# First key columns, gate tiles, RWKV's first operands and the last attention units, in a two-layer hybrid backbone step

## The chip, the cores and the metric

The kernel runs on one core of one Trainium2 chip. The metric is the device time of one launch in microseconds, the median of several runs.

## The reference, cut to what matters

One inference step of a two-layer backbone (width 1024) over 256 context tokens and 1024 latent tokens, 1280 rows in all, in float32.

```python
for i in range(2):                      # layer 0 even, layer 1 odd
    m = silu(cond) @ mod_w[i] + mod_b[i]            # shift, scale, gate (3 x 1024)
    h = rms_norm(x, norm_g[i]) * (1 + scale) + shift
    x = x + gate * mixer_i(h)
# even mixer: z = h @ w_in, split into
#   A: attention, 8 query heads of 64, 2 key heads, softmax over 512 cached
#      + 1024 latent + 256 context keys (context rows see only context)
#   B: RWKV-7, 8 heads of 64, both directions, each branch times a SiLU gate
#   concat(A, B) @ w_out
# odd mixer: gated linear attention, both directions, gate, @ w_out
# finally rms_norm
```

The change lies in the even mixer: in the passage from its projections to attention and RWKV, and in the order of attention's last pieces.

## The kernel before

**Stages.** Layer 0 first projects the normalised rows (`project_on`, L667) into queries, keys, values, gates and RWKV inputs, and stores all of them in DRAM (`qh_d`, `kh_d`, `vo_d`, `ga_d`, `gb_d`, `ws_d`, `vt_d`). Each float32 product of the projections is three products of split halves. Then the mixers run side by side: RWKV in 40 segments (`rwkv_seg`, L1381: 4 head pairs, 5 stretches of 256 rows, 2 directions), attention in 12 units (4 query-head pairs p4, 3 row groups g) and the remaining modulation columns as filler. Output projection, layer 1 and its output projection follow.

**Who sets the order.** The kernel carries its own planner, `Sched` (from L100). Every operation is a call that the planner holds back. Tasks are generators, grouped in streams (`drive`, L411). The planner estimates for the first instructions of each task when they could start, and issues the earliest (L470). At equal times the lower rank goes first: a stream's place in the list of `drive`, or, for streams with a share, a rank that they have in common and that grows with the TensorE time they have used. A stream with a lead is treated as if its start were that much earlier, except on SyncE. The engines then run their instructions in the order so fixed, and SyncE issues every DMA in that order; a transfer that must wait holds up all behind it. In what follows SPq is SyncE's issue queue. `get` (L369) takes a tile from a tag's free tiles and blocks until there is one, `put` gives it back, `until` waits on a condition in the planner's order, `then` sets a flag in it.

**Rooms.** SBUF is reused by stage. `room_attn` (L1239) waits until the projections but for the gates are done, makes the tiles of attention (KA and KB for each of two key heads, 1792 columns; VO; QA and QB, 4 each; `mw` and `m4`, one each, for modulation), loads the first head's KA, fills KB's other half on POOL (row 64 of KB is ones, the row that carries minus the row maximum in QB), loads `sT` and sets `attn`. `room_rwkv` (L1310) waits for the last gate's products and for two PSUM banks of the projections, makes the tiles of RWKV and its masks and constants, fills them (POOL memsets, then identity blocks into LL and Z by whichever of ScalarE and VectorE the planner prefers), and sets `rwkv`, for which every `rwkv_seg` waits before it takes its tiles and loads its operands AR, BK and Vs (256, 256 and two times 64 KB).

**Gates.** `gated` (L785) evicts a projected gate through a tile `gt` (two of them, L726): tanh on ScalarE, a product on VectorE, a store. `mod_cols` (L551), in the mixer stage called by `mods` (L1300) with 256 columns at a time, loads 1 MB of `mod_w` into `mw` and, for gate columns, a row of `mod_b` into a tile `gt`; it multiplies by sT, and stores the gate row.

**Attention.** `maxima` (L1678) goes through the units in order. Each unit has two halves (one query head each). For every half it loads QA (two issues) and QB, multiplies blocks of 128 queries with KA in chunks of 512 keys (`cw`), reduces each product's row maximum on VectorE, transposes the maxima on TensorE, negates them on ScalarE and sends them into row 64 of QB. A unit's maxima may run at most some 13 key tiles ahead of attention (`SLACK`, L1665). `attend` (L1718) starts when both halves are ready: score products KA x QA + KB x QB, exp on ScalarE, product with VO, sums on VectorE or POOL. It has one PSUM bank `po`, so one unit accumulates at a time. Units 10 and 11 are head pair 3 with the two groups of 512 latent rows. `room_norm` (L2306) waits for all units.

The streams of the mixers, with (tasks at once, share, lead):

```python
mixers = (((rwkv_norm(p, sts[p]) for p in range(4)), 1),
          ((rwkv_seg(...) for p in range(4) for step in range(5) for d in range(2)), 4, 2000, 0.15),
          (attention(maxima), 1, 60),
          (attention(attend), 2, 150), ([keys()], 1), ([mods()], 1))
```

Of the kernel before, what the change touches and what calls it, by code (L numbers as in the profile page):

```python
# [486 lines left out]
def tile_hybrid_dit_step(ctx: ExitStack, tc: tile.TileContext, I, C, O):  # L487
# [63 lines left out]
    def mod_cols(i, c0, n, bank, row, ready=lambda: True):  # L551
# [4 lines left out]
        for a in range(NK // nk):  # L556
# [19 lines left out]
        m4 = yield from get("m4", False)  # L576
# [14 lines left out]
        else:  # L591
            PE.matmul(p[0:2, :], lhsT=msel, rhs=m, start=True, stop=True)
            V.tensor_tensor(b[0:2, 0:n], p[0:2, :], b[0:2, 0:n], ALU.add)
            V.tensor_scalar(m[0:2, :], b[0:2, 0:n], 0.5, 0.0, ALU.mult, ALU.add)
            put(row, b)
# [122 lines left out]
    flags = dict(left=0, gates=0, attn=False, keys=0, rwkv=False, mods=False, normed=False, gla=False, gl=False, units=0, weights=0, lr=0, begun=0, ra=False)  # L718
# [21 lines left out]
    def layer0():  # L740
# [153 lines left out]
        def mods(n):  # L894

            yield from sch.until(lambda: loads[0] >= (5 if n % 2 else 1))
            yield from mod_cols(0, n * 512, 512, "a", "xr", lambda: modded[0] and modded[1])
# [341 lines left out]
    def room_attn():  # L1239
# [37 lines left out]
    def load_keys(v, x):  # L1277

        src = kh_d[64 * v:64 * v + 64, 0, :]
        if x == 0:  # L1280
            for h in range(2):
                D.dma_start(out=KA[v][64 * h:64 * h + 64, :].bitcast(F32), in_=kh_d[64 * v:64 * v + 64, h, :])
        else:
            D.dma_start(out=KB[v][0:64, :].bitcast(F32), in_=src)

    def keys():

        yield from sch.until(lambda: flags["attn"])
        def done():
            flags["keys"] += 1  # L1290

        load_keys(0, 1)
        D.dma_start(out=VO.rearrange("p t v d -> p t (v d)"), in_=vo_d)
        sch.then(done)
        yield from sch.until(lambda: attended[1] >= 2)
        for x in range(2):
            load_keys(1, x)
        sch.then(done)

    def mods():  # L1300
        yield from sch.until(lambda: flags["attn"])
        for i, c0 in ((0, 2 * DM), (1, 0)):
            for c in range(c0, 3 * DM, 256):
                yield from mod_cols(i, c, 256, "b", "gt")
# [5 lines left out]
    def room_rwkv():  # L1310
# [15 lines left out]
        D.dma_start(out=m1f, in_=C["k_m1"].rearrange("p (d c) -> p d c", d=2))  # L1326
        id16 = rc.tile([P, P], F16, name="id16")
# [10 lines left out]
        slots("y", 2, [P, T], pool=rn)  # L1338
        slots("AR", 3, [P, 3, 4, 64])
        slots("BK", 3, [P, 2, 4, 64])  # L1340
        slots("Vs", 3, [P, 2, 2, 64])
# [1133 lines left out]
```

## Time and profile before

| | us |
|---|---|
| median of 3 runs | 2081.95 (2080.56 to 2083.43) |
| the profiled execution | 2079.51 |
| its span, first to last instruction | 2077.7 |
| mean granted clock of TensorE | 0.987 |
| TensorE busy | 1991.9 (96%) |
| VectorE, ScalarE, POOL busy | 1453.5, 1007.2, 296.1 |

The profile was taken on one execution. PE is TensorE's products, PEld its weight loads, DVE VectorE, ACT ScalarE, SP SyncE. In it the projections of layer 0 end at 509.9 us, RWKV and attention run from there to about 1300, the rest is the output projection and layer 1. All operations go through one helper, so every row has the line of that helper (L357), and rows are told apart by their tiles: hhi, hlo, whi, wlo are the projections, AR to Xr RWKV, QA, KA, QB, KB, VO, mx, mr, pt, acc attention, mw, m, gate modulation. `pj` and `a` are PSUM banks.

### The profile page before, as it was taken

Reading aid. Unit: us, or ns where it says so; the run is one execution under the profiler, and the core shown is the slowest. Engines: PE = TensorE matmul, PEld = TensorE weight load, DVE = VectorE, ACT = ScalarE, POOL = GpSimd, SP = SyncE. Lnnn points to the kernel's source line nnn. Section 1 sums busy time; section 2 is a strip of 40 time slices with the busy share of each in tenths; the row PEclk is TensorE's granted clock in tenths of the full one; section 3 lists DMA queues with packets and bytes.
Section 4 is the critical chain, followed back from the end, with each engine's and each line's share of the span. In section 5 each row is a group of like instructions: output and inputs, shape, how many; then the busy total and the mean of one; then the engine's idle time right before and its main releaser. Section 6 shows DMA issues by size and latency. Waiting matters only on the chain.

```text
span 2077.7 us, 38540 instructions
## 1 busy us (share of the span) xinstructions
PE 1991.9 (96%) x14876; PEld 1554.9 (75%) x14876; DVE 1453.5 (70%) x2877; ACT 1007.2 (48%) x2181; POOL 296.1 (14%) x388
## 2 busy tenths in 40 slices
PE   6999999998899999999999998999999999999998
PEld 3878687886577777777777774788788888888886
DVE  4677866777887888888988888464575656564455
ACT  4455653553556646665656654153445454542111
POOL 2010200004221112111110111010121111110011
PEclk9999999999999989999999999999999999999999
DMA  8224342436613242223223214353101011115653
GB/s 300 71 102 160 132 164 90 166 102 217 196 49 112 65 143 74 77 78 120 67 80 92 70 55 139 117 172 90 35 22 56 29 49 34 44 33 171 188 173 111
DMA packets 215431, 220.61 MB, mean 106 GB/s; under 512 B 16512, under 2 KB 161264, under 8 KB 215248
## 3 DMA queue, kind: packets, MB, share of 16 engines
q1 hardware_dynamic: 215248, 218.15, 33.2%
q8 instruction: 117, 1.92, 0.4%
q14 instruction: 66, 0.54, 0.1%
HBM read 150.68 MB, written 67.39 MB: 105 GB/s over the span
## 4 chain that ended last, share of the span: by engine, by line
PE 55%; DVE 11%; issue 2%; ACT 2%; DMA 1%; SPq 0%; POOL 0%; POOLq 0%; DVEq 0%; ACTq 0%
PE a L357 31%; PE pj L357 24%; DVE QQ L357 2%; DVE mx L357 1%; DVE LL L357 1%; ACT QQ L357 1%; DVE TT L357 1%; DVE Z L357 1%; DVE dec L357 1%; DVE gt L357 1%; DVE y L357 0%; DVE GR L357 0%; DVE KX L357 0%; DVE acc L357 0%; DVE TR L357 0%
## 5 line engine op out<-in xcount | busy, mean ns | idle before, releaser
L357 PE MATMUL pj<-hhi,whi 128*128 128x512 f32 (+1 forms) x672 | 241.0, 361 | 2.6 <-DVE whi L357 1.4
L357 PE MATMUL pj<-hlo,whi 128*128 128x512 f32 (+1 forms) x672 | 241.2, 361 | 0.6 <-DVE hlo L357 0.6
L357 PE MATMUL pj<-hhi,wlo 128*128 128x512 f32 (+1 forms) x672 | 240.2, 359 | 1.6 <-DVE wlo L357 1.6
L357 PE MATMUL a<-h1hi,whi 128*128 128x512 f32 (+3 forms) x448 | 162.2, 363 | 0.0
L357 PE MATMUL a<-h1lo,whi 128*128 128x512 f32 (+3 forms) x448 | 161.7, 362 | 0.4 <-DVE h1lo L357 0.4
L357 PE MATMUL a<-h1hi,wlo 128*128 128x512 f32 (+1 forms) x424 | 153.7, 362 | 0.0
L357 PEld LDWEIGHTS pj<-hhi,whi 128*128 128x128 f32 x672 | 128.7, 192 | 26.4 <-issue 3.7
L357 PEld LDWEIGHTS pj<-hlo,whi 128*128 128x128 f32 x672 | 129.0, 192 | 23.8 <-issue 5.8
L357 PEld LDWEIGHTS pj<-hhi,wlo 128*128 128x128 f32 x672 | 128.8, 192 | 24.0 <-issue 4.1
L357 POOL TENSOR_TENSOR acc<-acc,pt 128x512 f32<-128x512 f32 (+1 forms) x57 | 72.4, 1278 | 379.2 <-ACT pt L357 221.9
L357 DVE TENSOR_TENSOR acc<-acc,pt 128x512 f32<-128x512 f32 (+1 forms) x127 | 93.1, 757 | 13.9 <-ACT pt L357 10.2
L357 PE MATMUL a<-pt,VO 128*64 128x512 f32 (+1 forms) x368 | 95.6, 602 | 0.3 <-ACT pt L357 0.3
L357 PE MATMUL a<-woh,oh 128*128 128x512 f32 (+1 forms) x248 | 91.8, 370 | 2.8 <-DVE oh L357 2.8
L357 PEld LDWEIGHTS a<-h1hi,whi 128*128 128x128 f32 (+1 forms) x448 | 83.3, 186 | 13.3 <-issue 0.4
L357 PEld LDWEIGHTS a<-h1lo,whi 128*128 128x128 f32 (+1 forms) x448 | 83.3, 186 | 13.2 <-DVE h1lo L357 0.8
L357 PE MATMUL a<-woh,ol 128*128 128x512 f32 (+1 forms) x248 | 91.5, 370 | 1.7 <-DVE ol L357 1.7
L357 PE MATMUL a<-wol,oh 128*128 128x512 f32 (+1 forms) x248 | 91.5, 369 | 0.0
L357 PEld LDWEIGHTS a<-h1hi,wlo 128*128 128x128 f32 x424 | 80.1, 189 | 11.2 <-DVE wlo L357 0.4
L357 POOL TENSOR_SCALAR sq<-sq 128x1 f32<-128x1 f32 x70 | 19.6, 280 | 479.6 <-ACT gt L357 195.3
L357 ACT ACTIVATE pt<-pj 128x512 f32<-128x512 f32 (+1 forms) x123 | 68.7, 593 | 35.4 <-PE pj L357 31.8
L357 DVE TENSOR_REDUCE mx<-pj 128x1 f32<-128x512 f32 (+1 forms) x117 | 74.2, 651 | 2.1 <-PE pj L357 2.1
L357 DVE TENSOR_REDUCE mx<-a 128x1 f32<-128x512 f32 x91 | 59.9, 672 | 9.6 <-PE a L357 9.5
(505 smaller groups left out, 5285.3 us busy)
## 6 DMA issues: line engine op xcount, KB each, us to landing
mw<-in_mod_w SPq DMA_DIRECT2D x24, 1024.0 KB
ws<-wk SPq DMA_DIRECT2D x32, 512.0 KB
wst<-in_ev_w_in SPq DMA_DIRECT2D x26, 512.0 KB
wst<-in_od_w_in SPq DMA_DIRECT2D x24, 512.0 KB
AR<-ws SPq DMA_DIRECT2D x40, 256.0 KB
BK<-ws SPq DMA_DIRECT2D x40, 256.0 KB
wst<-o SPq DMA_DIRECT2D x14, 512.0 KB
Vs<-vt SPq DMA_DIRECT2D x80, 64.0 KB
```

What stands on the lines that cost most here:

```text
L357: r = f(*a, **k)
```

## The change

Five edits. The first key head's KA is loaded in two parts: columns 0 to 511 in `room_attn`, the rest in `keys` after the first unit's first queries have been issued (`asked`); the first score may go before the rest (`ka`). `sT` is loaded after that, and `mods` waits for it. KB of the second head is filled when it is loaded, not at the start. `mod_cols` no longer takes a tile for the `mod_b` row but uses the second half of its own `m4` tile, which for gate columns it takes before the products. In `room_rwkv` the tiles y, AR, BK and Vs are made right after the masks, and a flag `segs` lets the segments load their operands then; their work still waits for `rwkv`. The fills of LL and Z go to ScalarE. Attention's units 10 and 11 form a stream of their own with a lead of 0.15 and no share.

```diff
-    def mod_cols(i, c0, n, bank, row, ready=lambda: True):
+    def mod_cols(i, c0, n, bank, ready=lambda: True):
...
             if a == 0 and c0 >= 2 * DM:
-                b = yield from get(row, False)
-                D.dma_start(out=b[0:2, 0:n], in_=I["mod_b"][i:i + 1, c0:c0 + n].to_broadcast([2, n]))
+                m4 = yield from get("m4", False)
+                b = m4[0:2, n:2 * n]
+                D.dma_start(out=b, in_=I["mod_b"][i:i + 1, c0:c0 + n].to_broadcast([2, n]))
...
-        m4 = yield from get("m4", False)
+        if c0 < 2 * DM:
+            m4 = yield from get("m4", False)
...
-            put(row, b)
...
 (room_attn)
-        load_keys(0, 0)
-        for v in range(2):
-            G.memset(KB[v][64:128, :].bitcast(F32), 0.0)
-            G.memset(KB[v][64:65, :].bitcast(F32), 1.0)
-        D.dma_start(out=sT.rearrange("p k c -> p (k c)"), in_=sT_d)
+        load_keys(0, 0, slice(0, 512))
+        fill_keys(0)
...
 (keys)
-        yield from sch.until(lambda: flags["attn"])
...
+        yield from sch.until(lambda: flags["attn"] and asked[0] >= 1)
+        load_keys(0, 0, slice(512, PAST + T))
+        sch.then(first)                       # sets flags["ka"]
+        D.dma_start(out=sT.rearrange("p k c -> p (k c)"), in_=sT_d)
+        sch.then(lambda: flags.__setitem__("sT", True))
         load_keys(0, 1)
         D.dma_start(out=VO.rearrange("p t v d -> p t (v d)"), in_=vo_d)
         sch.then(done)
         yield from sch.until(lambda: attended[1] >= 2)
+        fill_keys(1)
         for x in range(2):
             load_keys(1, x)
...
     def mods():
-        yield from sch.until(lambda: flags["attn"])
+        yield from sch.until(lambda: flags["sT"])
...
 (room_rwkv, after gmask, zmask and m1f are loaded)
+        slots("y", 2, [P, T], pool=rn)
+        slots("AR", 3, [P, 3, 4, 64])
+        slots("BK", 3, [P, 2, 4, 64])
+        slots("Vs", 3, [P, 2, 2, 64])
+
+        def loads():
+            flags["segs"] = True
+        sch.then(loads)
         id16 = rc.tile([P, P], F16, name="id16")
...
-                linear(x[:, :, 0, :], ident.unsqueeze(1).to_broadcast([P, 4, P]), -1.0)
+                S.mul(x[:, :, 0, :], ident.unsqueeze(1).to_broadcast([P, 4, P]), -1.0)
...
-                    copy(fv(x[:, 0, d * h:d * h + 1], ...), fv(id16[:, d * h:d * h + 1], ...))
+                    S.copy(fv(x[:, 0, d * h:d * h + 1], ...), fv(id16[:, d * h:d * h + 1], ...))
...
 (rwkv_seg)
-        yield from sch.until(lambda: flags["rwkv"])
+        yield from sch.until(lambda: flags["segs"])
...
         for e in range(2):
             D.dma_start(out=Vs[64 * e:64 * e + 64].rearrange("p j h k -> p j (h k)"), ...)
+        yield from sch.until(lambda: flags["rwkv"])
...
 (maxima, after the two QA issues)
+            if i == hh == 0:
+                def issued():
+                    asked[0] += 1
+                sch.then(issued)
...
                 for c in range(nch):
+                    yield from sch.until(lambda: c == 0 and k0 == 0 or flags["ka"])
...
-              (attention(attend), 2, 150), ([keys()], 1), ([mods()], 1))
+              (attention(attend, 0, 10), 2, 150), (attention(attend, 10), 2, None, 0.15), ([keys()], 1), ([mods()], 1))
```

## Rows read from the trace of the kernel before

**Rows 1.** The page's part 1: busy time of each engine, its share of the span, and the number of instructions.

```profile
PE 1991.9 (96%) x14876; PEld 1554.9 (75%) x14876; DVE 1453.5 (70%) x2877; ACT 1007.2 (48%) x2181; POOL 296.1 (14%) x388
```

**Rows 2.** The view by stretches of 5 us around the passage from the projections to the mixers. Columns: stretch (us), its length, busy time and number of instructions of PE, PEld, DVE, ACT and POOL, mean granted clock of TensorE, mean busy share of the DMA engines, GB/s.

```profile
505.00:510.00 5.00, 4.90 (x22) 3.74 (x20) 0.66 (x2) 0.23 (x1) 3.72 (x3) 1.00 0.96 296
510.00:515.00 5.00, 0.04 (x1) 0.07 (x1) 0.00 (x0) 0.00 (x0) 4.98 (x8) 0.81 1.07 233
515.00:520.00 5.00, 5.00 (x12) 3.69 (x12) 4.24 (x8) 0.00 (x0) 5.00 (x10) 0.50 0.97 306
520.00:525.00 5.00, 1.99 (x18) 0.68 (x17) 4.84 (x17) 2.59 (x7) 0.50 (x2) 0.84 1.09 307
525.00:530.00 5.00, 4.59 (x21) 2.48 (x13) 4.97 (x16) 1.94 (x8) 2.69 (x10) 0.82 0.49 173
530.00:535.00 5.00, 2.72 (x21) 1.13 (x22) 5.00 (x12) 0.20 (x1) 0.00 (x0) 0.86 1.08 358
535.00:540.00 5.00, 4.62 (x42) 3.67 (x40) 3.59 (x10) 2.75 (x7) 2.27 (x3) 0.80 0.73 214
540.00:545.00 5.00, 3.24 (x32) 2.38 (x33) 4.18 (x11) 3.15 (x7) 0.59 (x1) 1.00 0.70 226
```

**Rows 3.** The timeline: start and length in us, engine, line, operation, output <- inputs, shapes, number; in brackets the engine's idle time just before and what ended it. The first keys and queries, the first score, the first row maximum.

```profile
506.25 1.11 SPq L357 DMA_DIRECT2D KA<-kh  x2
508.03 1.08 SPq L357 DMA_DIRECT2D QA<-qh  x2
...
514.96 0.77 PE L357 MATMUL a<-KA,QA 128*128 128x512 f32 x1 [5.06 <-DMA QA<-qh]
...
515.76 0.69 DVE L357 TENSOR_REDUCE mx<-a 128x1 f32<-128x512 f32 x1 [7.86 <-PE a L357]
```

**Rows 4.** The DMA view. The first line is what the engines moved in 40 equal slices (1.125 us each) of the stretch from 500 to 545 us; the others are issues by kind in it or in the stretch from 490 to 600: number, KB each.

```profile
GB/s 15 107 382 322 337 379 273 248 236 230 175 240 287 204 204 350 384 381 356 351 260 240 372 209 0 53 334 389 363 366 304 340 309 224 27 146 87 153 323 383
...
KA<-kh SPq DMA_DIRECT2D x2, 448.0 KB
...
sT<-sT_d SPq DMA_DIRECT2D x1, 128.0 KB
...
QA<-qh SPq DMA_DIRECT2D x8, 128.0 KB
...
AR<-ws SPq DMA_DIRECT2D x3, 256.0 KB
```

**Rows 5.** The timeline again: the key tiles' fills on POOL, the modulation's bias row into a gt tile, and the last gate's eviction on ScalarE.

```profile
502.35 6.43 POOL L357 MEMSET KB<- 64x1792 f32 x4
...
505.83 0.33 SPq L357 DMA_DIRECT2D gt<-in_mod_b  x1
...
520.41 0.60 ACT L357 ACTIVATE gt<-pj 128x512 f32<-128x512 f32 x1 [15.18 <-DMA gb<-gt]
```

**Rows 6.** The timeline: the last of POOL's fills of the RWKV room, the first constant on VectorE, and Z copies on ScalarE and on VectorE.

```profile
519.59 0.52 POOL L357 MEMSET Z<- 128x512 f16 x1
...
523.74 0.22 DVE L357 CAST id<-ident 128x128 f16<-128x128 f32 x1
...
524.05 1.02 ACT L357 COPY Z<-id 128x256 f16<-128x256 f16 x3 [2.00 <-DVE hm L357]
...
524.96 0.71 DVE L357 COPY Z<-id 128x256 f16<-128x256 f16 x4
```

**Rows 7.** The timeline: SyncE's issues of the second half's queries, of the last mask, of QB's row and of the first RWKV operand, and the first RWKV product.

```profile
513.71 3.52 SPq L357 DMA_DIRECT2D QA<-qh  x2
...
519.62 0.33 SPq L357 DMA_DIRECT2D gsq<-in_k_m  x1
...
526.77 0.69 SPq L357 DMA_DIRECT2D QB<-mr  x1
...
528.00 0.58 SPq L357 DMA_DIRECT2D AR<-ws  x1
...
534.64 0.58 PE L357 MATMUL a<-AR,BK 64*128 64x128 f32 x1
```

**Rows 8.** The timeline: the last maximum of the second half, its negative copy, the issue of QB's row, and the second half's first attention product.

```profile
534.14 0.14 DVE L357 TENSOR_REDUCE mx<-mx 128x4 f32<-128x12 f32 x1
...
534.80 0.27 ACT L357 ACTIVATE mr<-a 4x128 fp32r<-4x128 f32 x1 [7.83 <-PE a L357]
...
537.47 0.66 SPq L357 DMA_DIRECT2D QB<-mr  x1
...
542.11 0.47 PE L357 MATMUL pj<-QA,KA 128*128 128x512 f32 x1
```

**Rows 9.** The view by stretches of 10 us at the end of the mixers (columns as in Rows 2), and from the timeline the longest wait in them.

```profile
1240.00:1250.00 10.00, 9.37 (x38) 4.39 (x37) 9.59 (x14) 7.21 (x12) 3.86 (x3) 1.00 0.65 204
1250.00:1260.00 10.00, 8.43 (x30) 3.72 (x28) 9.97 (x12) 7.97 (x12) 3.98 (x3) 1.00 0.56 165
1260.00:1270.00 10.00, 6.05 (x20) 3.44 (x21) 10.00 (x15) 2.78 (x5) 5.11 (x2) 0.87 0.55 168
1270.00:1280.00 10.00, 10.00 (x40) 4.00 (x39) 7.50 (x13) 5.62 (x11) 0.00 (x0) 0.95 0.58 188
...
1267.91 0.80 PE L357 MATMUL pj<-QA,KA 128*128 128x512 f32 x1 [3.18 <-DVE mx L357]
```

**Rows 10.** The view by stretches of 20 us, one stretch in the middle of the mixers (columns as in Rows 2).

```profile
740.00:760.00 20.00, 17.03 (x167) 13.42 (x163) 18.59 (x38) 6.73 (x20) 3.44 (x4) 0.89 0.30 83
```

More of the change, by code (lines that the diff above doesn't have):

```diff
@@ L592, in mod_cols @@
             PE.matmul(p[0:2, :], lhsT=msel, rhs=m, start=True, stop=True)
-            V.tensor_tensor(b[0:2, 0:n], p[0:2, :], b[0:2, 0:n], ALU.add)
-            V.tensor_scalar(m[0:2, :], b[0:2, 0:n], 0.5, 0.0, ALU.mult, ALU.add)
-            put(row, b)
+            V.tensor_tensor(b, p[0:2, :], b, ALU.add)
+            V.tensor_scalar(m[0:2, :], b, 0.5, 0.0, ALU.mult, ALU.add)
             D.dma_start(out=gate_d[i][:, c0 - 2 * DM:c0 - 2 * DM + n], in_=m[0:2, :])
@@ L717, in tile_hybrid_dit_step @@
     left, segs, right = (ctx.enter_context(ExitStack()) for i in range(3))
-    flags = dict(left=0, gates=0, attn=False, keys=0, rwkv=False, mods=False, normed=False, gla=False, gl=False, units=0, weights=0, lr=0, begun=0, ra=False)
+    flags = dict(left=0, gates=0, attn=False, keys=0, rwkv=False, mods=False, normed=False, gla=False, gl=False, segs=False, ka=False, sT=False, units=0, weights=0, lr=0, begun=0, ra=False)
     def pool(stack, name, **k):
@@ L896, in mods @@
             yield from sch.until(lambda: loads[0] >= (5 if n % 2 else 1))
-            yield from mod_cols(0, n * 512, 512, "a", "xr", lambda: modded[0] and modded[1])
+            yield from mod_cols(0, n * 512, 512, "a", lambda: modded[0] and modded[1])
             def done():
@@ L1275, in room_attn, with fill_keys, load_keys @@
         sch.then(done)
-    def load_keys(v, x):
+    def fill_keys(v):
+        G.memset(KB[v][64:128, :].bitcast(F32), 0.0)
+        G.memset(KB[v][64:65, :].bitcast(F32), 1.0)
+    def load_keys(v, x, cs=slice(0, PAST + T)):
         src = kh_d[64 * v:64 * v + 64, 0, :]
@@ L1281, in load_keys @@
             for h in range(2):
-                D.dma_start(out=KA[v][64 * h:64 * h + 64, :].bitcast(F32), in_=kh_d[64 * v:64 * v + 64, h, :])
+                D.dma_start(out=KA[v][64 * h:64 * h + 64, cs].bitcast(F32), in_=kh_d[64 * v:64 * v + 64, h, cs])
         else:
@@ L1286, in keys, with first @@
     def keys():
-        yield from sch.until(lambda: flags["attn"])
+        def first():
+            flags["ka"] = True
         def done():
             flags["keys"] += 1
+        yield from sch.until(lambda: flags["attn"] and asked[0] >= 1)
[3 more added lines that the diff above has]
+        sch.then(lambda: flags.__setitem__("sT", True))
         load_keys(0, 1)
@@ L1300, in mods @@
     def mods():
-        yield from sch.until(lambda: flags["attn"])
+        yield from sch.until(lambda: flags["sT"])
         for i, c0 in ((0, 2 * DM), (1, 0)):
             for c in range(c0, 3 * DM, 256):
-                yield from mod_cols(i, c, 256, "b", "gt")
+                yield from mod_cols(i, c, 256, "b")
         def done():
@@ L1337, in room_rwkv @@
         V.tensor_tensor(id2, ident[:, 0:64], ident[:, 64:128], ALU.add)
[L1338 to L1341, printed above, removed]
         slots("BT", 2, [P, 4, P])
@@ L1359, in room_rwkv @@
                 for x in sch.slot[f"Z{l}{d}"]:
-                    copy(fv(x[:, 0, d * h:d * h + 1], [[P, 4], [2 * h, 64 // h], [1, h]]),
-                         fv(id16[:, d * h:d * h + 1], [[0, 4], [2 * h, 64 // h], [1, h]]))
+                    S.copy(fv(x[:, 0, d * h:d * h + 1], [[P, 4], [2 * h, 64 // h], [1, h]]),
+                           fv(id16[:, d * h:d * h + 1], [[0, 4], [2 * h, 64 // h], [1, h]]))
         slots("GH", 2, [P, 2, 2 * SEG])
@@ L1665, in tile_hybrid_dit_step @@
     SLACK = 13
+    asked = [0]
     halves = [slice(64 * hh, 64 * hh + 64) for hh in range(2)]
@@ L1788, in tile_hybrid_dit_step, with attention @@
     order = ((0, 1, 2, 3, 4), (0, 4, 3, 2, 1))
-    def attention(f):
-        for i, (p4, g) in enumerate(units):
+    def attention(f, a=0, b=12):
+        for i, (p4, g) in list(enumerate(units))[a:b]:
             yield f(i, p4, g)
```

## The prediction

> **What bounds the kernel now.** First the page's busy shares [rows 1]: TensorE is busy 96% of 2077.7 us and no other engine comes near, so the time is TensorE's work plus the stretches in which it idles or runs below full clock. The view by stretches then says where those lie, and the change touches two of them.
>
> The first is the passage from the projections to the mixers [rows 2]. From 510 to 545 us TensorE idles 4.96, 0.00, 3.01, 0.41, 2.28, 0.38 and 1.76 us of each 5: 12.8 us. After the 4.96 us of idle it is granted 0.50, the 1.2 GHz level, from 515 to 520, and it is back at 2.4 GHz for good only after 540. Busy time times the missing share of the clock (5.00 x 0.50, 1.99 x 0.16, 4.59 x 0.18, 2.72 x 0.14, 4.62 x 0.20) comes to about 4.9 us. Some 17.7 us is all that this passage can give.
>
> The second is the end of the mixers [rows 9]: 0.63, 1.57 and 3.95 us idle between 1240 and 1270, and about 1.3 us of clock (6.05 x 0.13 + 10 x 0.05). VectorE is busy 9.6 to 10 us of 10 there, and the longest wait is 3.18 us for a row maximum.
>
> Between the two there is little to gain: once attention and RWKV both run, TensorE is filled. So what starts earlier at 540 should arrive earlier at the end.
>
> **The chain through the passage.** The timeline gives it [rows 3]. KA is issued at 506.25, the queries at 508.03, the first score runs at 514.96 after a 5.06 us wait, and VectorE reduces from 515.76, having stood idle for 7.86 us. The last maximum of the second half is ready at 534.14, its negative copy starts at 534.80, the transfer that puts it into QB is issued only at 537.47, and the second half's attention starts at 542.11 [rows 8]. RWKV starts at 534.64, on operands issued at 528.00 [rows 7]. These two starts are what the change can move.
>
> **Keys' first columns.** Before: KA 2 x 448 KB, sT 128 KB, queries 2 x 128 KB: 1280 KB stand ahead of the first score [rows 4]. After: 2 x 128 KB of KA (512 of 1792 columns) and the queries, 512 KB. The two stretches from 505 to 515 moved 296 and 233 GB/s [rows 2], 265 in the mean, so 768 KB less is up to 2.9 us for the first score. But only the first 512 columns of the first query block may go ahead. The second score needs the other 2 x 320 KB, and ahead of it then lie 512 + 640 KB and probably the 128 KB of QB: 1280 KB again. What is won is one reduction off the chain, 0.69 us [rows 3]. I take **0.6 us**, between 0 (if the first score waits for the whole tile after all) and 2.9. The two added issues take about 0.55 us each on SyncE (1.11 us for two) [rows 3], where sT, KB and VO now wait behind them; none of these is what TensorE waits for at 514.96, so I cost that at nothing; uncovered it is those 1.1 us.
>
> A page speaks against the split: the Trainium skill, "DMA: Bandwidth & Descriptors", section Measured, asks for 1 MiB transfers and gives 138 GB/s at 64 KB against 341 at 1 MB. By it 256 KB of KA in small pieces would cost an estimated 1.1 us more, and the sum below would end 1.1 us later. The trace does not show that: beside transfers of 128 to 448 KB the queue holds over 300 GB/s in many slices.
>
> **Gates keep their own tiles.** At 505.83 the mod_b row takes one of the two gt tiles, so the last gate's evictions must share the other. ScalarE waits for the store of the previous result and stands 15.18 us, until 520.41 [rows 5]. All of ScalarE's program stands behind it, and the gate product on VectorE and the mixers' constants behind it (523.74) are late with it [rows 6]. With the row in m4's second half this wait goes. Next late is the projection's own end at 509.9, where TensorE's stand of 5.06 us before 514.96 begins [rows 3]: the eviction runs then, in VectorE's idle 7.86 us. The modulation blocks now hold m4 from their load on, so the next row waits for the previous gate transfer. They are fillers and I cost this at nothing; without that cover it would be one transposed product late per block, below 1 us.
>
> **Fills on ScalarE.** POOL still fills until 520.1 (519.59 + 0.52) and is not shortened. VectorE loses its Z copies, 0.18 us each (0.71 for four); ScalarE gains them at 0.34 us each (1.02 for three) [rows 6]. With the constants ahead of the reductions instead of among them, and these fills gone, I estimate 3 to 4 us off VectorE's chain between 523 and 534: the gate product, the constants and the copies that stand there now. ScalarE is free for them once the 15.18 us wait is gone. If it does not go, the first half's negative copy is late behind them, by ten copies, 3.4 us.
>
> **RWKV's first operands.** The loads move from behind "all fills done" to just behind the masks (519.62), past QB's row (526.77) on SyncE [rows 7]. The DMA line shows what for: about 527 us the engines fall to 0 and 53 GB/s for two slices of 1.1 us while SyncE waits [rows 4]. Each segment brings 256 + 256 + 128 KB in four issues, three segments 1920 KB. Issued about 520 behind a queue that was full until 526, its 640 KB at 0.33 MB per us are through by 528, and with 1 to 2 us for completion (my estimate) its first product can run about 529 to 530 instead of 534.6: 4.6 to 5.6 us. Attention's second half gains the 3 to 4 us on VectorE, and up to 2.4 us because QB's row (535.07 to 537.47) no longer waits behind operand loads [rows 8].
>
> So both starts move 5 us, and idle time after 520 falls from 7.8 us (3.01 + 0.41 + 2.28 + 0.38 + 1.76) to about 3.5. I take **4.4 us** together for gates, fills and operands. Bounds: nothing, or 5 us lost (the third rival), against all 7.8 us and the 2.4 us of clock after 520.
>
> **Half the key fills later.** Two of the four KB fills, half of 6.43 us on POOL [rows 5], move behind the second finished unit. POOL is busy 14% of the span [rows 1], so I cost it at nothing; uncovered it is 3.2 us for one of POOL's additions.
>
> **Last units first.** Units 10 and 11 get 0.15 us of lead, as RWKV has, over maxima, weight splitting and output projection, on VectorE and ScalarE too. TensorE's work stays the same; what can shrink is the 6.15 us of idle and 1.3 us of clock [rows 9]. But VectorE is full there, and a lead changes its order, not its total; unit 11's maxima, which get no lead, must still precede its attention. I take a third of the idle, **2.0 us**, between 7.4 gained and 3.2 lost (one more wait like the longest).
>
> **Sum:** 0.6 + 4.4 + 2.0 = 7.0 us. The profiled execution took 2079.51 us, 1.8 more than its span, and goes to 2072.5; it stands 2.4 us below the median of 2081.95, which goes to **2075.0**. About 0.2%, 4.2 us, is what a measurement can tell from no change: faster means below 2077.8, slower above 2086.1.
>
> **Rivals.**
> **1. As above**, 2069 to 2077.7: chance 0.50. For it: the hole in the DMA line and the 15.18 us wait are both removed by the edits named.
>
> **2. The gain is given back**, 2078 to 2086, likeliest 2081: chance 0.24. The kernel's order is planned greedily and any early shift rearranges 700 us of it. A stretch such as 740 to 760, where TensorE idles 2.97 us and the clock falls to 0.89 [rows 10], can come or go by itself and eat 5 us. Against it: most of that stage has no such hole.
>
> **3. The operand loads get in front of attention**, about 2087: chance 0.14. The planner gives SyncE to RWKV before maxima at equal times. If the loads are issued ahead of the second half's queries (513.71 before) [rows 7], these land 1920 KB later, 6.4 us at 0.3 MB per us, and so does attention's start. Of that I let RWKV's own work cover 1.4 us, 5 us remain. It decides if that query issue follows the first AR issue. Against it: the queries are asked early and the masks stand between.
>
> **4. Both passages give nearly all**, 2063 to 2069: chance 0.12. First gap 2.9, then 7.8 and 2.4 after 520, a third of the end: about 15 us, 2067.
>
> That the first columns do not help at all costs only 0.6 us and is inside 1.
>
> **Numbers.** Faster holds cases 1 and 4, 0.62; same is case 2, 0.24; slower is case 3, 0.14. The range 2066 to 2086 leaves out case 3 and half of case 4, 0.20.
>
> **What would show it.** Right: ScalarE's wait before the last gate under 4 us; AR and BK on SyncE near 520 and the first RWKV product near 529; the second half's attention near 537; less than 9 us of TensorE idle from 510 to 545; 1240 to 1275 with under 4 us idle. Wrong: the second half's queries issued after AR; the first score moved but the second not earlier than before with the same idle behind it; idle of 3 us at a new place between 560 and 1200; unit 11's maxima waiting alone.

## The result, and the profile after

The changed kernel takes 2102.70 us (median of 4 runs, 2101.06 to 2106.45); the kernel before 2081.26 (median of 4 runs, 2078.00 to 2083.43). The ratio is 1.0116, 95% interval 1.0096 to 1.0137: 21 us slower, where 7 us faster was forecast. The profiled execution spans 2099.3 us against 2077.7.

First, where the time lies. Over the span, TensorE's idle time and its busy time times the missing share of the clock were summed from the view by stretches of 10 us (5 us from 500 to 560), in us as idle / clock:

| stretch | before | after |
|---|---|---|
| 0–500 | 31.8 / 5.8 | 32.0 / 7.1 |
| 500–560 (the passage) | 13.3 / 5.0 | 17.7 / 6.3 |
| 560–900 | 8.0 / 6.5 | 5.9 / 0.0 |
| 900–1200 | 6.0 / 0.0 | 5.0 / 0.0 |
| 1200–1400 (the end of the mixers) | 10.1 / 1.3 | 22.9 / 10.3 |
| 1400–1900 | 4.5 / 0.0 | 5.4 / 0.0 |

The passage lost 6 us where it was to gain 5, the middle gained 10, and the end of the mixers lost 22. These sums are an estimate and can be some us off: in p1_before_lead13 below they come to 43.8 us from 0 to 500 against 37.6 before, and yet its first score runs 0.6 us sooner (514.35).

**The passage.** The timeline of the changed kernel, the rows that answer to [rows 3] and [rows 5 to 8]:

```profile
511.58 0.60 ACT L357 ACTIVATE gt<-pj 128x512 f32<-128x512 f32 x1 [4.74 <-PE pj L357]
511.66 1.85 POOL L357 MEMSET UV<- 128x1024 f32 x2 [4.46 <-PE pj L357]
512.37 0.47 PE L357 MATMUL a<-KA,QA 128*128 128x512 f32 x1 [0.83 <-ACT gt L357]
512.81 9.01 DVE L357 CAST id<-ident 128x128 f16<-128x128 f32 x1
...
516.13 1.19 PE L357 MATMUL pj<-KA,QA 128*128 128x512 f32 x2 [3.29 <-DMA KA<-kh]
...
518.26 0.62 SPq L357 DMA_DIRECT2D AR<-ws  x1
519.36 2.38 POOL L357 MEMSET Z<- 128x512 f16 x5
...
523.69 0.68 DVE L357 TENSOR_REDUCE mx<-a 128x1 f32<-128x512 f32 x1
...
530.37 1.24 SPq L357 DMA_DIRECT2D QA<-qh  x2
534.87 0.58 PE L357 MATMUL a<-AR,BK 64*128 64x128 f32 x1
...
568.72 0.50 PE L357 MATMUL a<-QA,KA 128*128 128x512 f32 x1
```

The last gate's eviction waits 4.74 us instead of 15.18, the first score comes 2.6 us earlier, and RWKV's first operands are issued at 518.26 instead of 528.00. None of it arrives. The cast that took 0.22 us at 523.74 [rows 6] now runs at 512.81, amid POOL's train of 16 fills, and stands until the train is over: 9.01 us. The first maximum comes at 523.69 (515.76 before [rows 3]). The second half's queries are issued at 530.37, behind all three segments' operands (513.71 before [rows 7]). RWKV's first product is where it was (534.64 before), and the first attention product runs at 568.72. Before, the first one, of the first half, ran at 537.23, and the second half's at 542.11 [rows 8]. The kernel before:

```profile
537.23 0.48 PE L357 MATMUL a<-QA,KA 128*128 128x512 f32 x1
```

The view by 5 us of the changed kernel (columns as in [rows 2]) shows the clock: behind TensorE's waits of 0.83 us before 512.37 and 3.29 us before 516.13 the 1.2 GHz level is granted from 515 to 535, where before it was for one stretch of 5 us (515 to 520):

```profile
515.00:520.00 5.00, 2.90 (x6) 1.82 (x6) 5.00 (x1) 0.69 (x2) 5.00 (x10) 0.50 1.05 303
520.00:525.00 5.00, 0.58 (x1) 0.29 (x1) 4.79 (x17) 3.09 (x9) 4.01 (x13) 0.50 1.05 363
525.00:530.00 5.00, 2.60 (x5) 1.15 (x4) 5.00 (x9) 1.10 (x4) 0.58 (x2) 0.50 0.96 335
530.00:535.00 5.00, 3.31 (x21) 0.90 (x21) 1.46 (x5) 1.45 (x4) 0.00 (x0) 0.50 0.63 205
```

**The end of the mixers.** The view by 10 us (columns as in [rows 2], answering to [rows 9]):

```profile
1250.00:1260.00 10.00, 10.00 (x40) 4.49 (x41) 9.56 (x14) 8.49 (x14) 1.46 (x1) 1.00 0.55 161
1260.00:1270.00 10.00, 5.92 (x14) 2.55 (x12) 9.97 (x13) 2.87 (x4) 0.91 (x1) 0.78 0.42 131
1270.00:1280.00 10.00, 6.29 (x14) 3.07 (x13) 9.01 (x18) 0.27 (x1) 0.00 (x0) 0.67 0.43 121
1280.00:1290.00 10.00, 6.78 (x18) 4.08 (x19) 4.02 (x8) 3.85 (x7) 0.00 (x0) 0.52 0.31 102
...
1330.00:1340.00 10.00, 4.61 (x24) 3.28 (x22) 5.99 (x9) 4.55 (x11) 1.17 (x1) 0.87 0.43 154
1340.00:1350.00 10.00, 8.08 (x28) 6.76 (x29) 2.50 (x5) 3.41 (x9) 0.62 (x2) 0.62 0.37 110
```

Which work stands there is read from SyncE's issues in the timeline. `AR<-ws` is an RWKV segment's operand load (the last one is shown), `QB<-mr` the row that ends the maxima of half a unit, `o<-ga` the store that ends a unit of attention, `o<-y` a store of RWKV's last normed rows. The kernel before; its units 9, 10 and 11 are the three `o<-ga`:

```profile
1191.44 0.32 SPq L357 DMA_DIRECT2D AR<-ws  x1
1217.01 0.33 SPq L357 DMA_DIRECT2D o<-ga  x1
...
1244.90 0.58 SPq L357 DMA_DIRECT2D QB<-mr  x1
...
1272.43 0.58 SPq L357 DMA_DIRECT2D QB<-mr  x1
...
1276.97 0.32 SPq L357 DMA_DIRECT2D o<-ga  x1
1282.81 0.32 SPq L357 DMA_DIRECT2D o<-y  x1
1324.70 0.32 SPq L357 DMA_DIRECT2D o<-ga  x1
```

and the changed kernel, with the longest waits of TensorE between:

```profile
1177.06 0.33 SPq L357 DMA_DIRECT2D AR<-ws  x1
...
1221.99 0.43 SPq L357 DMA_DIRECT2D o<-ga  x1
...
1263.94 0.33 SPq L357 DMA_DIRECT2D o<-ga  x1
...
1272.95 0.37 PE L357 MATMUL a<-ident,mx 128*4 128x128 f32 x1 [2.59 <-DVE mx L357]
1273.65 0.58 SPq L357 DMA_DIRECT2D QB<-mr  x1
...
1283.45 0.59 SPq L357 DMA_DIRECT2D QB<-mr  x1
1284.26 0.32 SPq L357 DMA_DIRECT2D o<-y  x1
...
1314.50 0.33 SPq L357 DMA_DIRECT2D o<-ga  x1
...
1341.92 1.97 PE L357 MATMUL a<-ident,xt 128*128 128x128 f32 x8 [6.63 <-DVE xt L357]
```

RWKV's last operands are loaded 14 us sooner and attention's unit 9 ends 5 us later. Unit 10 has the lead and ends 13 us sooner; unit 11's maxima run behind it, with next to no other work for TensorE beside them, at VectorE's pace, and its attention starts when they are done. Later the tiles of the output have no work beside them and TensorE waits 6.63 us for the chain that makes the next one, which ends on VectorE. In the middle TensorE is as full as before; what changed there is whose work it did. A number for that, picked when the runs were known, **attention's lag**, is the store of unit 9 less the issue of RWKV's last operand load: 1217.01 − 1191.44 = 25.6 us before, 1221.99 − 1177.06 = 44.9 us after.

### The profile page after: what moved, and what is told of

Same layout as the page of the kernel before. It is cut to its first block, busy times and chain, and to the rows that moved or that the text cites. A ratio compares the mean times of both kernels' runs of the same rounds, so it can differ in the third digit from the quotient of the medians.

```text
span 2099.3 us, 38575 instructions
## 1 busy us (share of the span) xinstructions
PE 1998.3 (95%) x14876; PEld 1557.1 (74%) x14876; DVE 1451.5 (69%) x2868; ACT 1016.0 (48%) x2201; POOL 280.4 (13%) x377
## 4 chain that ended last, share of the span: by engine, by line
PE 47%; DVE 11%; issue 2%; ACT 2%; DMA 1%; SPq 0%; POOL 0%; POOLq 0%; DVEq 0%; ACTq 0%
PE pj L357 27%; PE a L357 20%; DVE QQ L357 2%; DVE mx L357 2%; ACT QQ L357 1%; DVE LL L357 1%; DMA x<-xt 1%; DVE dec L357 1%; DVE gt L357 1%; DVE Z L357 1%; DVE TT L357 1%; DVE KX L357 0%; DVE y L357 0%; DVE GH L357 0%; DVE Ad L357 0%
## 5 line engine op out<-in xcount | busy, mean ns | idle before, releaser
L357 PE MATMUL pj<-h1hi,whi 128*128 128x512 f32 (+3 forms) x448 | 164.7, 369 | 0.0
L357 PE MATMUL pj<-h1lo,whi 128*128 128x512 f32 (+3 forms) x448 | 164.0, 367 | 0.0
L357 PE MATMUL pj<-h1hi,wlo 128*128 128x512 f32 (+1 forms) x432 | 159.4, 369 | 0.0
L357 PEld LDWEIGHTS pj<-hhi,wlo 128*128 128x128 f32 x672 | 129.1, 192 | 23.9 <-issue 4.1
L357 PEld LDWEIGHTS pj<-h1hi,whi 128*128 128x128 f32 (+1 forms) x448 | 83.7, 187 | 13.7 <-DVE gt L357 0.8
L357 PEld LDWEIGHTS pj<-h1lo,whi 128*128 128x128 f32 (+1 forms) x448 | 83.8, 187 | 12.1
L357 PEld LDWEIGHTS pj<-h1hi,wlo 128*128 128x128 f32 x432 | 81.6, 189 | 11.5
L357 PE MATMUL pj<-woh,ol 128*128 128x512 f32 (+1 forms) x232 | 85.7, 369 | 1.0 <-DVE ol L357 1.0
L357 PE MATMUL pj<-wol,oh 128*128 128x512 f32 (+1 forms) x232 | 85.6, 369 | 0.0
L357 PE MATMUL pj<-woh,oh 128*128 128x512 f32 (+1 forms) x232 | 85.4, 368 | 0.0
L357 ACT COPY ring<-pj 64x64 f32<-64x64 f32 x206 | 42.4, 206 | 48.4 <-PE pj L357 42.1
```

Source lines behind the costliest of these rows:

```text
L357: r = f(*a, **k)
```

## The experiments

All were timed against the kernel before on the same chip; the ratio with its interval is what is compared. The three right columns are read from SyncE's issues as above: the lag, the issue of unit 11's second `QB<-mr`, and unit 11's store. A pace number is RWKV's lead (0.15) or SLACK (13); "no copy forms" means that VectorE's copies in RWKV's set-up are written as another instruction (experiments one and two). The kernels are sorted by the lag.

| run | what it is | ratio (95%) | lag | unit 11's maxima | unit 11 over |
|---|---|---|---|---|---|
| p3_after_pace | changed, one stream, no copy forms, two pace numbers | 1.0010 (1.0001–1.0020) | 23.9 | 1254.5 | 1288.9 |
| e4_before_last | before, last units first alone | 1.0091 (1.0074–1.0109) | 25.5 | 1279.1 | 1309.9 |
| (before) | | 1 | 25.6 | 1272.4 | 1324.7 |
| p4_late_pace | as f7, one pace number | 0.9977 (0.9967–0.9987) | 28.2 | 1258.4 | 1313.8 |
| p1_before_lead13 | before, one pace number | 1.0112 (1.0095–1.0129) | 43.7 | 1274.1 | 1369.2 |
| q1_hold_tiles | changed, one stream, no copy forms, tiles held | 1.0115 (1.0100–1.0130) | 44.9 | 1276.4 | 1307.4 |
| p6_last_only | changed, no copy forms, lead for unit 11 alone | 1.0086 (1.0071–1.0101) | 44.9 | 1278.2 | 1313.0 |
| f3_stt_all | changed, no copy forms | 1.0110 (1.0095–1.0125) | 44.9 | 1279.1 | 1309.8 |
| e3_one_stream_stt | changed, one stream, id16 no copy | 1.0151 (1.0134–1.0169) | 44.9 | 1279.5 | 1376.9 |
| e1_one_stream | changed, one stream | 1.0157 (1.0140–1.0175) | 44.9 | 1279.7 | 1377.0 |
| e2_stt | changed, id16 no copy | 1.0120 (1.0100–1.0140) | 44.9 | 1283.3 | 1314.5 |
| (after) | | 1.0116 (1.0096–1.0137) | 44.9 | 1283.5 | 1314.5 |
| p5_early_alone | before, early operand loads alone | 1.0117 (1.0100–1.0134) | 49.3 | 1280.7 | 1376.7 |
| f6_late_stt | changed, late loads, no copy forms | 1.0184 (1.0167–1.0201) | 75.4 | 1353.6 | 1382.6 |
| f7_late_stt_one | as f6, one stream | 1.0197 (1.0181–1.0214) | 75.4 | 1310.7 | 1384.7 |
| p2_gate_alone | before, the gates' own tiles alone | 1.0200 (1.0185–1.0215) | 75.4 | 1313.9 | 1387.9 |
| f1_late_loads | changed, late loads | 1.0202 (1.0187–1.0218) | 75.4 | 1356.3 | 1385.3 |

### One: the split, and the copy that stands

The first theory, L, was that giving the last units the lead is what loses; its rivals put the loss on the passage.

e1_one_stream, the changed kernel with attention in one stream:

```diff
-              (attention(attend, 0, 10), 2, 150), (attention(attend, 10), 2, None, 0.15), ([keys()], 1), ([mods()], 1))
+              (attention(attend), 2, 150), ([keys()], 1), ([mods()], 1))
```

> The changed kernel with attention's units 10 and 11 back in the one attention stream; all else as changed, and the order of every engine is the changed kernel's until unit 10. Theory L (the lead lets unit 10's attention run out ahead of unit 11's maxima, which then run alone): the 13.0 us of TensorE idle between 1260 and 1290 and its 1.2 GHz stretch shrink to about 4 us, time 2102.7 - 12 to 16 = 2087 to 2091. Rival (the end is late because the passage at 510 to 545 put RWKV and attention out of step, whatever the order of the last units): the idle at the end stays above 9 us, time 2098 to 2103.

Measured 2110.65 us, slower than the changed kernel and outside both. e4_before_last is the split alone, on the kernel before:

> The kernel before with only the split of attention's stream (units 10 and 11 with a lead of 0.15). Theory L: unit 11's maxima run alone after unit 10's attention, idle of 10 to 14 us between 1240 and 1300 against 6.2 before, time 2081.3 + 5 to 12 = 2086 to 2093. Rival (the split is harmless without the passage's shift): 2077 to 2083.

Measured 2096.26: the direction of L at more than its size. Unit 10 ends at 1257.21 (1276.97 before), unit 11's maxima are done only at 1279.13 (1272.43). So the split costs 0.91% where attention is on time and saves 0.4% (1.0157 to 1.0116) where it is late. L alone does not hold.

e2_stt writes id16 with an instruction that is no copy, in the changed kernel; e3_one_stream_stt does so in e1:

```diff
-        V.tensor_copy(id16, ident)
+        V.scalar_tensor_tensor(out=id16, in0=ident, scalar=1.0, in1=ident, op0=ALU.mult, op1=ALU.max)
```

> The changed kernel with one instruction exchanged: the constant id16 is written on VectorE by a scalar_tensor_tensor (ident times 1, maximum with ident) in place of a copy; every other instruction keeps its place, but for one swap on ScalarE. In the changed kernel that copy is recorded with 9.01 us, 512.81 to 521.82, and POOL's train of fills ends at 521.74. Theory P (the copy form stands until POOL's train is over, a form with two inputs does not): the instruction takes 0.2 to 0.4 us, the first reduction comes at about 513.5 instead of 523.69 and the last of the second half 5 to 7 us earlier; time 2102.7 - 4 to 8 = 2095 to 2099. Rival (the instruction waits for the space that POOL's fills or the last projection release, whatever its form): the new one ends about 521.8 too, time 2101 to 2104.

> Both: one attention stream and id16 by scalar_tensor_tensor. Theories L and P together: 2102.7 - 16 to 24 = 2079 to 2087, near the kernel before (2081.3). If the early RWKV loads also cost (the second half's queries are issued at 530.37 instead of 513.71), it stays at 2083 to 2087; if all the rest of the change works as it was forecast, 2076 to 2079. Rivals of L and P: above 2092.

Measured 2102.67 and 2109.09, the times of the kernels that they were made from. VectorE's timeline in e2 says why: the new form runs through amid POOL's fills, and the next copy stands instead.

```profile
512.85 0.28 DVE L357 SCALAR_TENSOR_TENSOR id<-ident 128x128 f16<-128x128 f32 x1
...
513.65 9.22 DVE L357 COPY ring<-id 64x64 f32<-64x64 f32 x9
```

### Two: late queries (theory Q) or the standing copy (theory S)

f1_late_loads puts RWKV's operand loads back behind its set-up; f3_stt_all rewrites the ring tiles' copies as e2 does id16 (all sixteen on VectorE; seven had been POOL's), with TensorE's and SyncE's order unchanged; f6_late_stt is both; f7_late_stt_one is f6 with one stream.

```diff
 def rwkv_seg(p, d, seg, st, step):
-        yield from sch.until(lambda: flags["segs"])
+        yield from sch.until(lambda: flags["rwkv"])
```

and in f3, beside e2's line (in0 and in1 are the same half of id2):

```diff
-                pcopy(ring[q][i][64 * (1 - q % 2):64 * (1 - q % 2) + 64, :], id2[64 * (1 - q % 2):64 * (1 - q % 2) + 64, :])
+                V.scalar_tensor_tensor(out=ring[q][i][...], in0=id2[...], scalar=1.0, in1=id2[...], op0=ALU.mult, op1=ALU.max)
```

> The changed kernel with one part undone: RWKV's operand loads wait again for the end of its set-up, so the second half's queries go out ahead of them; stream split, gate tiles, key split and fills as changed. Theory Q (attention starts 31 us late because those queries stand behind 1.9 MB of operand loads, and that lateness is paid at the end): second half's queries issued below 522, the first attention products below 550 (568.7 in the changed kernel), RWKV's first product at 535 to 540. The split of the last units is still there and by itself cost 18 us on the kernel before, so the time stays at 2088 to 2098. Rival S (the copy that VectorE stands on for 9 us is the cause): queries earlier but the first attention product still above 560, time 2099 to 2105.

> The changed kernel with every VectorE copy of RWKV's set-up (id16 and the ring tiles) written as a two-input scalar_tensor_tensor of the same values; the order of the matmuls and of the DMA issues is the same. Theory Q: the 9 us on one VectorE instruction go, the first half's maxima end 6 to 8 us earlier, but the second half's queries stay behind the operand loads and attention still starts above 558; 2094 to 2102. Rival S: the stall is the cause, attention moves 8 us or more ahead and the time falls to 2080 to 2092.

> Both together: operand loads at the end of the set-up and no copy form on VectorE in it; the stream split stays. Theory Q: first attention product below 542 (537 in the kernel before); what is left is the split's own cost, 2084 to 2096. Rival S: as in the run without the copies, 2080 to 2092, and then the loads make no difference between the two.

> The same with attention in one stream again, so of the change the gate tiles, the key split and the fills on ScalarE are left. Theory Q with the split's cost: attention on time and no split, so the end looks as before; 2070 to 2079, as fast as or faster than the kernel before (2078). Rival (the list order at the end is what any change upsets, whatever its place): 2085 to 2100.

All but f3, which came out as Q said (2098.74, attention at 561.62), missed. In f1 the queries went out early, and the time grew to 2118.67; the first attention product came at 554.21, not below 550. SyncE's issues:

```profile
518.89 2.59 SPq L357 DMA_DIRECT2D QA<-qh  x2
...
533.56 0.57 SPq L357 DMA_DIRECT2D AR<-ws  x1
```

f3 took the standing copy away: RWKV's first product ran at 525.94, 9 us sooner, and the first maximum at 514.53. All units of attention end some 7 us sooner up to unit 9 (1214.98 against 1221.99), the last one 4.7, and the profiled span is 2094.7 against 2099.3. Of these shifts 1.5 us are there before the passage (the first queries are issued at 506.96 against 508.50). So in these two executions, where the order stays, a passage that is 5.5 us shorter arrives with some 3 us at the end. The ratios against the kernel before, 1.0110 and 1.0116, can't be told apart. f6 and f7 have neither late queries nor a standing copy and are among the slowest, 2114.55 and 2115.90. Q and S both fall. In each of the three with late loads most of the loss sits from 1200 us on, as in the changed kernel, and the lag had gone to 75.4 us.

### Three: the order of the mixed stage (theory R)

Theory R has the passage only as the cause of another order. The kernel's planner writes down every engine's order from its own estimates, and each part that shifts a start in the passage makes it deal out TensorE between RWKV and attention anew for the next 700 us. p1_before_lead13 tests that without any part of the change, by one number of the planner; p2_gate_alone has one of the parts that the prediction counted as a gain, the gates' own tiles; p3_after_pace and p4_late_pace change pace numbers of kernels that had lost. The values of those numbers were chosen among the orders that the planner writes for lead and slack around 0.15 and 13, so the runs show that such a number can bring the loss or take it away, not that any other value would.

p1 on the kernel before, and p4 on f7 with 0.11:

```diff
-               4, 2000, 0.15),
+               4, 2000, 0.13),
```

p2 on the kernel before, cut to its core:

```diff
-                b = yield from get(row, False)
+                m4 = yield from get("m4", False)
+                b = m4[0:2, n:2 * n]
...
-            put(row, b)
```

p3 on e3, with the ring tiles as in f3:

```diff
-    SLACK = 13
+    SLACK = 14
...
-               4, 2000, 0.15),
+               4, 2000, 0.1),
```

> The kernel before with one number changed and no part of the change in it: RWKV's lead in the written-out order 0.13 instead of 0.15. The passage at 500 to 560 us keeps its instructions. Theory R (the loss is a race at the end of the mixed stage: if unit 10's attention ends before RWKV's last normed rows come, unit 11's attention takes TensorE first; if it ends after them, the first output tiles do, unit 11 ends only at about 1370 and the last group's tiles wait for it; any change of the order around can tip it): unit 10 ends after the last rows, unit 11's last store at 1360 to 1385 (1325 in the kernel before), time 2096 to 2108. Rivals Q and S (the loss comes from the passage's late queries or its standing copy): the passage is as before, 2072 to 2084.

> The kernel before with the gates' own tiles alone (keys whole, no early operand loads, fills as before, one stream). Theory R: RWKV starts some us earlier at 527 to 532, the race tips, unit 11's last store at 1370 to 1390, time 2100 to 2116: this part alone loses what the whole change loses. Rivals Q and S and the prediction's own step (the part gains up to 4 us by itself): 2070 to 2080.

> The earlier run of one stream without copy forms on VectorE (2109) with the two numbers that pace attention against RWKV changed, lead 0.15 to 0.10 and slack 13 to 14; all parts of the change in the passage stay (key split, gate tiles, early operand loads, fills on ScalarE), late queries too. Theory R: attention keeps up, unit 10 ends before or with RWKV's last rows, unit 11's last store below 1330, time 2074 to 2088. Rivals Q and S: late queries are still there, 2100 to 2112.

> The earlier run with operand loads at the end of the set-up, one stream and no copy forms (2115.9) with RWKV's lead 0.11 instead of 0.15, nothing else. Theory R: unit 11's last store at 1315 to 1330 and 2066 to 2080, as fast as the kernel before or faster by the 4 us of the passage. Rivals: one number of the order moves nothing of the passage, 2108 to 2118.

The times are 2100.69, 2119.17, 2079.33 and 2073.90: three in R's ranges, p2 3 us past it, and all four on R's side of the rivals. In p2 R was wrong about the way, though: RWKV did not start earlier, at 527 to 532, but later, at 538.69. There, too, VectorE's copies stood amid POOL's fills (1.67 and 5.63 us), and the sums as in the first table come to 26.6 us from 500 to 560 against 18.3 before. So some 8 of p2's 42 us are the passage's own. p1, in which TensorE's order is that of the kernel before up to 542 us and both starts lie within 2 us of where they were, loses what the change loses. SyncE's issues, with TensorE's longest wait:

```profile
1180.99 0.33 SPq L357 DMA_DIRECT2D AR<-ws  x1
...
1224.66 0.32 SPq L357 DMA_DIRECT2D o<-ga  x1
...
1274.07 0.60 SPq L357 DMA_DIRECT2D QB<-mr  x1
1277.80 0.32 SPq L357 DMA_DIRECT2D o<-y  x1
1278.40 0.32 SPq L357 DMA_DIRECT2D o<-ga  x1
1369.18 0.32 SPq L357 DMA_DIRECT2D o<-ga  x1
1376.44 0.80 PE L357 MATMUL pj<-woh,oh 128*128 128x512 f32 x1 [10.03 <-DVE oh L357]
```

RWKV's rows are complete at 1277.80, before unit 10 is; the first output tiles then run ahead of unit 11, which ends at 1369.18, and the last tiles wait 10.03 us for it. p4 is f7 with that one number, and its issues are again those of a kernel without the loss:

```profile
1182.58 0.33 SPq L357 DMA_DIRECT2D AR<-ws  x1
...
1210.80 0.39 SPq L357 DMA_DIRECT2D o<-ga  x1
...
1258.36 0.58 SPq L357 DMA_DIRECT2D QB<-mr  x1
...
1265.80 0.32 SPq L357 DMA_DIRECT2D o<-ga  x1
...
1278.97 0.33 SPq L357 DMA_DIRECT2D o<-y  x1
1313.82 0.32 SPq L357 DMA_DIRECT2D o<-ga  x1
```

Its idle time and clock from 1200 to 1400 are 3.8 / 0.0 us (10.1 / 1.3 before), in the passage 14.0 / 6.4 (13.3 / 5.0). At 0.9977 it is faster than both kernels, and not by the passage. How much of that its parts bring can't be said: the kernel before was run with one other pace number only, the 0.13 of p1. p3 has the gate tiles, the key split, the early loads and the late queries (issued at 530.27, behind the operands at 518.21, 525.50 and 527.89), and comes to 1.0010: late queries alone do not bring the 21 us.

### Four: what was still open

q1_hold_tiles asks whether the loss is only that output tiles go ahead of unit 11. It is the changed kernel with one stream and no copy forms, and it holds the output tiles back:

```diff
 def out_tile(i, tt, src, finish):
+        if i == 0:
+            yield from sch.until(lambda: attended[1] >= 12)
```

> The changed kernel with attention in one stream and no copy forms on VectorE in RWKV's set-up (2109 with only id16 rewritten), and the first output tiles held until unit 11's attention is over; everything up to 1280 us keeps its order. Theory R, narrow (the loss is only who gets TensorE first at the end, and unit 11's attention behind the tiles is what costs): unit 11 ends near 1310 and the time falls to 2082 to 2094. Theory R, wide (attention is late against RWKV; with the tiles second they stand alone afterwards and TensorE waits for their VectorE part, so the gap only moves): unit 11 ends near 1310 as well, but the time stays at 2098 to 2110.

Measured 2104.49, the wide reading. Unit 11 is over at 1307.39, and the gap is where the tiles then stand alone; TensorE's longest wait:

```profile
1346.04 1.97 PE L357 MATMUL a<-ident,xt 128*128 128x128 f32 x8 [10.85 <-DVE xt L357]
```

p6_last_only gives the lead to unit 11 alone, in f3's kernel:

```diff
-              (attention(attend, 0, 10), 2, 150), (attention(attend, 10), 2, None, 0.15), ([keys()], 1), ([mods()], 1))
+              (attention(attend, 0, 11), 2, 150), (attention(attend, 11), 2, None, 0.15), ([keys()], 1), ([mods()], 1))
```

p5_early_alone is the kernel before with the early loads: the tiles of y, AR, BK and Vs made ahead of id16, and

```diff
 def rwkv_seg(p, d, seg, st, step):
-        yield from sch.until(lambda: flags["rwkv"])
+        yield from sch.until(lambda: flags["segs"])
...
+        yield from sch.until(lambda: flags["rwkv"])
         pair(AR[:, 2], id2.unsqueeze(1).to_broadcast([P, 4, 64]), last.to_broadcast([P, 4, 64]), ALU.mult)
```

> The changed kernel without copy forms (2098.7), the lead given to unit 11's attention alone instead of to units 10 and 11. If the split costs because unit 10's attention goes ahead of unit 11's maxima and leaves them alone: unit 11's second maxima stored before 1283, 2086 to 2096. If any lead of the last units costs the same: 2097 to 2103.

> The kernel before with the early operand loads alone. Wide theory R: this order also puts attention late, 2098 to 2112, with unit 11's last store at 1360 to 1385. Only the gate tiles bring the loss: 2072 to 2084.

p6 measured 2098.00, in the range of the second reading by its time; by its ratio, 1.0086 against 1.0110 for f3 with overlapping intervals, there may be some 5 us in it. Its maxima are done at 1278.19, before 1283 as the first reading had it, but f3's were done at 1279.11 already, so that sign could not tell the two apart. That stays undecided. p5 measured 2105.15 with unit 11 over at 1376.70, as R said: this part alone also loses.

Read down, the table says two things. In one stream the lag sorts the time: below 29 us 0.998 to 1.001, at 43.7 to 49.3 us 1.011 to 1.016, at 75.4 us 1.020. And the kernels with a loss all have unit 11's maxima later than 1273, those without it earlier, though by little: 1272.4 in the kernel before, 1274.1 in p1. The lag is set by the gate tiles, the early loads and the pace number: kernels that share these have the same lag to 0.1 us, whatever the copy form, the split, the key split and the fills do. That the order written for the mixed stage decides is shown by p1 and p4, where one pace number alone took the time up or down, and by p3, which has the ring's copies rewritten besides. In the three, the lag moved with the time; no run moved the lag and nothing else, so it is a mark of such an order, and that it rules the end is argued. It is not all of it either: e4 loses 0.91% at 25.5 us, by its split, and p5 at 49.3 us loses less than e1 at 44.9. Which of the planner's choices between 560 and 1200 us makes 44.9 or 75.4 of 25.6 was not followed, and the key split and the fills on ScalarE were not run alone. f7 has them and one stream as p2 has, which lacks them, at 1.0197 and 1.0200; but f7 has no copy forms either.

## Why the prediction was wrong

**The step that failed** is the sentence that carried the sum from the passage to the end: TensorE is filled once both mixers run, so what starts earlier at 540 "should arrive earlier at the end". It holds in part for a given order (f3: 5.5 us of the passage, some 3 us of span). It does not hold for a change that makes the planner write another one. TensorE was as full after as before from 560 to 1200 us (10.9 us idle against 14.0), but what it did there had changed. A full engine was taken as proof that nothing could be lost in that stretch. What was lost is the mixture left for the end, 22 us from 1200 to 1400.

A second step failed ahead of it, and alone would have cost the forecast its gain: "both starts move 5 us". Neither did. RWKV started at 534.87 instead of 534.64, attention at 568.72 instead of 537.23, and the passage lost 6 us. This step is the smaller one: f3, with RWKV starting at 525.94, still loses 1.10%, and p3, with attention starting at 561.92, loses 0.10%.

**Rival 2 was the mechanism, mis-sized.** It said that any early shift rearranges 700 us of the order, and priced that as one hole like [rows 10], 5 us, inside "same". The runs show no hole in the middle; the price falls due at the end, where unit 11's maxima or the last tiles stand alone: 1.1 to 1.2% (p1, p5, after) or 2.0% (p2, f1), 21 to 42 us. [rows 9] held a warning of it: VectorE is full there and TensorE waits for it, so whatever maxima are still to do when RWKV is over run at VectorE's pace (0.68 us for each reduction; the changed kernel had 24 of them left). Attention's own products do not: from 1290 to 1320 TensorE is busy all the time in the changed kernel.

**Rival 3 happened and was not the cause.** Its sign, the query issue behind the first AR, came true (530.37 against 518.26), attention started 31 us late, and the end was slower. But with the queries early the loss grew (f1, 1.0202), and with them late it went (p3, 1.0010).

By its terms:
- **Keys' first columns, 0.6:** the first score moved 2.6 us, the second waited for the rest, as said. The one reduction was lost to the standing cast. Nothing of it was singled out in the time.
- **Gates, fills, operands, 4.4:** the 15.18 us wait went, as worked out, and the operands were issued 1.7 us before the forecast 520. What the step missed is what that wait had done: it kept VectorE's copies off POOL's train of fills. The first RWKV product stayed at 534.87 instead of 529 to 530. With the copies rewritten it ran at 525.94 (f3), so RWKV's half of the mechanism was right; attention's half was not, it started at 561.62 even then, behind the late queries. The gate tiles alone cost 2.0%, the early loads alone 1.2%, both with a longer lag, and by the sums some 8 us of the former lie in the passage.
- **Half the key fills, 0:** nothing speaks against it.
- **Last units first, 2.0:** on the kernel before it costs 0.91%, 18 us. The sentence that unit 11's maxima "must still precede its attention" was the mechanism; the bound of 3.2 us allowed one such wait, and there were 24 maxima with next to no other work for TensorE beside them (from 1259.53 to 1282.47 in the changed kernel).

Of the four signs named as wrong, three came: queries behind AR, the second score not earlier (516.13 against 515.52), unit 11's maxima alone. The fourth, idle of 3 us at a new place between 560 and 1200, did not: TensorE's longest wait there is 1.38 us.

## What to carry to other kernels

Where a planner writes the order of a long stage with two kinds of work on one engine, a local gain ahead of that stage is not a term of a sum. First ask what the stage leaves for its end, and follow one number for that (here the lag of attention behind RWKV) through every variant. Before you credit or blame a part, change a pace number alone: if that moves the time as much as the part does, only a comparison with each side's pace chosen again tells what the part is worth. And ask of a wait that you remove what it kept apart.

## What the runs showed of the hardware

A VectorE copy or cast that comes amid a train of POOL fills can stand through many of them. In the changed kernel a 128x128 cast of 0.22 us stood 9.01 us. In e2 nine 64x64 copies took 9.22 us, the first of them 8.18. In p2 two Z copies stood 5.63 us. Each of these waits ended with the train. The end of the train is not always what frees it: p2's cast came free after 1.67 us, at 511.91, with fills running on to 519.24. Why it did stays open. Beside POOL's TENSOR_SCALAR on the ring tiles, right behind the train, no copy stood: nine took 1.43 us (changed kernel, 522.34). VectorE and POOL in p2:

```profile
510.24 1.67 DVE L357 CAST id<-ident 128x128 f16<-128x128 f32 x1
...
513.75 5.63 DVE L357 COPY Z<-id 128x256 f16<-128x256 f16 x2 [1.38 <-POOL Z L357]
...
516.86 2.38 POOL L357 MEMSET Z<- 128x512 f16 x5
```

A scalar_tensor_tensor of the same values took 0.28 us in the same place, and sixteen of 64x64 took 2.56 us together (f3). The Trainium skill, "SBUF — State Buffer", section "Who interferes with whom", has the form of this: copies and casts may take a port pair that VectorE shares with GpSimd, and a two-input instruction contends only with one that reads SBUF, which a fill does not. The trace agrees on the forms. On the length it differs: there the one that loses waits for the other's instruction, while here each fill took 0.48 to 0.93 us and the copy waited for several of them in a row, in three of the four cases for all that were left.
